# Routing an expert layer by bf16 one-hot matmuls, and one weight subtraction moved behind two products

## Chip, core and metric

The kernel runs on one core of a Trainium2 chip. Its time is the device time of one execution in microseconds (us), as the median over executions. TensorE (PE in the rows, its weight loads PEld), VectorE (DVE), ScalarE (ACT), GpSimd (POOL) and SyncE (SP) work side by side and wait for each other through semaphores.

## The reference

One layer over 1024 latent tokens of width 1024, with 256 context tokens in front. A token mixer (input projection, a spatial-gating half, a recurrent half, output projection) is followed by a mixture of 16 experts. All inputs are float32. What matters here is the second part:

```
aff = softmax(h @ w_r)                    # 1024 tokens x 16 experts
gate, idx = top_k(aff.T, 128)             # each expert chooses 128 tokens
xe = h[idx]
hid = silu(xe @ w1) * (xe @ w3)           # w1, w3: 1024 x 2048 for each expert
ye = (hid @ w2) * gate                    # w2: 2048 x 1024
out = rmsnorm(x + g2 * zeros.at[idx].add(ye))
```

## The kernel before

**First stages.** Up to about 430 us the kernel computes the modulation, the mixer and the router logits. Tiles that live through the kernel lie in the pool `con` on the left side of SBUF; the working tiles of these stages lie in pools on the right side, above a filler tile `edge_pad`. A second filler, `gap_pad`, lies on the left, just below the pool `mb` of the expert loop. The fillers are never used; they only set the addresses of what follows.

**Sorting and places.** Each expert's 128th largest score is found by a sort on VectorE, whose steps stand in the list `fills` and are issued one by one. From the thresholds, lines L1189 to L1205 compute `pos`: the place (0 to 127) that a token has in an expert's list, or a number out of range.

**Routing.** `route_oh(e)` compares `pos` with 0..127 on VectorE, which gives eight one-hot blocks of 128 x 128 in fp32r. `route(e)` multiplies them, as stationary operands, with `tvr`: for each token and expert four fp32r columns (token number, score rounded to fp32r, the rest of the score, token number again). The eight matmuls add up in PSUM; VectorE turns column 0 into an integer (L1230) and adds columns 1 and 2 into the gate (L1231). GpSimd then gathers the rows with an indirect DMA.

**Expert loop.** Weights come in pieces of 1 MB (128 x 2048, float32), 24 for each expert, into a ring of 12 buffers, by DMAs that SyncE issues as buffers come free. ScalarE rounds a piece to fp32r (`hi`, L107), VectorE subtracts (`lo`, L109), and TensorE multiplies hi by hi, hi by lo and lo by hi (L1258, L1260, L1262 in `up`; L1301, L1304, L1307 in `down`). The split of a piece is issued two pieces ahead (`presplit`, LA = 2), into three buffers for `hi` and `lo`. For each expert e the order is `up("3", e)`, `hidden(e)`, `up("1", e + 1)`, `down(e)`. `up` fills four PSUM banks over eight pieces; in its first piece it takes the banks in two halves, (0, 1) and (2, 3). `hidden` multiplies the four banks with the stored silu on VectorE, and so frees them. Since TensorE has six banks in all, the second half of the next `up` needs two banks that `hidden` frees. `route(e + 2)` is issued after piece 6 of `up("3", e)`. So the order on VectorE around that place is: subtractions of pieces up to the next `up`'s piece 0, the two small operations of `route`, the subtraction of piece 1, four products, the subtractions of pieces 2 and 3.

Of the kernel before, what the change touches and what calls it, by code (L numbers as in the profile page):

```python
# [7 lines left out]
F32 = mybir.dt.float32  # L8
F32R = mybir.dt.float32r
BF = mybir.dt.bfloat16  # L10
I32 = mybir.dt.int32
AF = mybir.ActivationFunctionType
OP = mybir.AluOpType
AX = mybir.AxisListType
# [4 lines left out]
NE = 16  # L19
FE = 2048  # L20
P = 128
# [3 lines left out]
LA = 2  # L25
# [20 lines left out]
def hybrid_layer(ctx, tc, x, c, ctxt, c_ctx, w_mod, b_mod, norm1_g, norm2_g, w_in, sgu_g, sgu_w,  # L46
# [3 lines left out]
    V, A, PE, G = nc.vector, nc.scalar, nc.tensor, nc.gpsimd  # L50
# [7 lines left out]
    con = ctx.enter_context(tc.tile_pool(name="con", bufs=1))  # L58
# [11 lines left out]
    def bank(shape, name, small=0):  # L70
        return banks[small].tile(shape, F32, name=name, tag="bk")
# [30 lines left out]
    def presplit(n, eng, pool=None, defer=None):  # L102
        while nsplit[0] < min(len(units), n):
            s = units[nsplit[0]][1]
            hi = (pool or sp).tile([P, 2048], F32R, name="hi")
            lo = (pool or sp).tile([P, 2048], F32R, name="lo")
            A.activation(hi, s, AF.Copy)  # L107
            if defer is None:
                eng.tensor_tensor(lo, s, hi, op=OP.subtract)  # L109
            else:  # L110
                defer.append(lambda lo=lo, s=s, hi=hi: eng.tensor_tensor(lo, s, hi, op=OP.subtract))
            ready[nsplit[0]] = (hi, lo)
            nsplit[0] += 1

    def unit(key):
        n = nused[0]
        nused[0] += 1
        assert units[n][0] == key
        presplit(n + 1 + LA, V)
        return ready.pop(n)  # L120

    plan("1", w1, 0)
# [3 lines left out]
    ph1 = ExitStack()  # L126
    wbs, bps, p0s = ExitStack(), ExitStack(), ExitStack()
    edge = wbs.enter_context(tc.tile_pool(name="edge", bufs=1, side="right"))
    edge.tile([P, 56], F32, name="edge_pad")
    wb = wbs.enter_context(tc.tile_pool(name="wb", bufs=2, side="right"))  # L130
    bp = bps.enter_context(tc.tile_pool(name="bp", bufs=1, side="right"))
    p0 = p0s.enter_context(tc.tile_pool(name="p0", bufs=1, side="right"))
# [30 lines left out]
    for q in range(4):  # L163
# [9 lines left out]
    iota_s = con.tile([P, P], F32, name="iota_s")  # L173
    G.iota(iota_s, pattern=[[1, P]], base=0, channel_multiplier=0,
           allow_small_or_imprecise_dtypes=True)
    tv = con.tile([P, 8, NE, 2], F32, name="tv")
    G.iota(tv[:, :, :, 0], pattern=[[P, 8], [0, NE]], base=0, channel_multiplier=1,
           allow_small_or_imprecise_dtypes=True)
    for r0, n_, src in ((72, 8, rg_lam.rearrange("o d (b p) -> (o d b) p", p=P)),
                        (80, 8, rg_ba.rearrange("o d (b p) -> (o d b) p", p=P)),  # L180
                        (88, 8, rg_bi.rearrange("o d (b p) -> (o d b) p", p=P)),
# [119 lines left out]
    for k in range(8):  # L301
        hi = p0.tile([P, 2048], F32R, name="mhi", bufs=2)
        lo = p0.tile([P, 2048], F32R, name="mlo", bufs=2)
        for c0, n_ in (((0, 4),) if k < 7 else ((0, 1), (1, 1), (2, 1), (3, 1))):
# [3 lines left out]
            for w in (hi, lo):  # L308
                for n in range(c0, c0 + n_):
                    PE.matmul(pm[n], cs4[:, k, :], w[:, n * 512:(n + 1) * 512],  # L310
                              start=(k == 0 and w is hi), stop=(k == 7 and w is lo))
# [18 lines left out]
    for j in range(16):  # L330
# [8 lines left out]
                           op0=OP.add, op1=OP.mult)  # L339
# [343 lines left out]
    pr = ph1.enter_context(tc.tile_pool(name="pr", bufs=1))  # L683
# [160 lines left out]
    p = bank([P, 4, P], "ws")  # L844
# [30 lines left out]


    pes = ExitStack()
    pe_ = pes.enter_context(tc.tile_pool(name="pe", bufs=1, side="right", reuse_waits="tile"))

    A2 = pe_.tile([P, D], F32, name="A2row")  # L880
# [16 lines left out]
    def x_load(t):  # L897
        XR[t] = pe_.tile([P, D], F32, name="xr", bufs=2)
        nc.sync.dma_start(XR[t], x[t * P:(t + 1) * P])

    x_load(0)
    x_load(1)
    affs = tv[:, :, :, 1]

    groups = ((0,), (1, 2), (3, 4), (5,), (6, 7))
    WS, SS = [[pe_.tile([64, 64], F32, name=f"{c_}{i}") for i in range(2)] for c_ in "WS"]
# [3 lines left out]
    V.tensor_scalar(tri, jp, 0.0, None, op0=OP.is_gt)  # L910
    oneb = pe_.tile([P, P], BF, name="oneb")
    G.memset(oneb, 1.0)
    for v in pre:
        G.memset(v, 0.0)
    def out_mm(t, h, ks=range(4), ns=(0, 1)):
# [15 lines left out]
    fills = []  # L931
# [14 lines left out]
    def wait2():  # L946
        fills.append(done2[0] + len(fills2))
# [62 lines left out]
    def router_w(t):  # L1010

        i = [t == g_[-1] for g_ in groups]
        if not any(i):
            return
        i = i.index(True)
        n = NE * len(groups[i])
        pt = bank([n, P], "pt")
        PE.transpose(pt, affs[:, groups[i][0]:t + 1].rearrange("p t e -> p (t e)"), ident)
        for h in range(2):
            A.activation(WS[i][32 * h:32 * h + n], pt[:, h * 64:(h + 1) * 64], AF.Copy)  # L1020
# [48 lines left out]
    for t in range(1, 8):  # L1069
# [4 lines left out]
        if t in (4, 6):  # L1074
            i = t // 2 - 1
# [59 lines left out]
    fill(1)  # L1135
    ph1.close()

    tvr = ctx.enter_context(tc.tile_pool(name="tvp", bufs=1)).tile([P, 8, NE, 4], F32R, name="tvr")
    sp = ctx.enter_context(tc.tile_pool(name="sp", bufs=LA + 1))
    res_add(7, 1)  # L1140
    nc.sync.dma_start(x2d[7 * P:], xr)
# [19 lines left out]
    del fills[:]  # L1161
    router_sm(7)
    router_w(7)
    A.activation(tvr[:, :, :, 1], affs, AF.Copy)
    for i in (0, 3):
        A.activation(tvr[:, :, :, i], tv[:, :, :, 0], AF.Copy)
    q_sort(4, L5)
    LZ = LS[0]
    fills.insert(8, lambda: V.tensor_sub(tvr[:, :, :, 2], affs, tvr[:, :, :, 1]))
    wait2()  # L1170
    q_merge(LS[1], L5, LZ)
    while fills:
# [36 lines left out]
    mp = ctx.enter_context(tc.tile_pool(name="mp", bufs=1))  # L1209
    xe, ix, xT, sg, hT = {}, {}, {}, {}, {}  # L1210

    OH = {}

    def route_oh(e):
        oh = mp.tile([P, 8, P], F32R, name="oh", tag="xe", bufs=2)
        n = 1 if e else 2
        for h in range(n):
            ts = slice(8 // n * h, 8 // n * (h + 1))
            V.tensor_tensor(oh[:, ts], iota_s[:, None, :].to_broadcast([P, 8 // n, P]),
                            pos[:, ts, e:e + 1].to_broadcast([P, 8 // n, P]), op=OP.is_equal)  # L1220
        OH[e] = oh

    def route(e):
        oh = OH.pop(e)
        p = bank([P, 4], "pr", 1)
        for t in range(8):
            PE.matmul(p, oh[:, t], tvr[:, t, e, :], start=(t == 0), stop=(t == 7))
        i = mp.tile([P, 1], I32, name="ix", bufs=4)
        g = mp.tile([P, 1], F32, name="gate", bufs=4)
        V.tensor_copy(i, p[:, 0:1])  # L1230
        V.tensor_reduce(g, p[:, 1:3], axis=AX.X, op=OP.add)  # L1231
        if e == NE - 1:
            V.tensor_copy(ixf, p[:, 0:1])
        ix[e] = (i, g)
        xe[e] = mp.tile([P, D], F32, name="xe", bufs=2)
        G.indirect_dma_start(out=xe[e], out_offset=None, in_=hx2d,  # L1236
                             in_offset=bass.IndirectOffsetOnAxis(ap=i[:, :1], axis=0))
# [13 lines left out]
    def up(which, e, mid):  # L1251
        pt = [bank([P, 512], "h" + which) for _ in range(4)]
        hi, lo = xT[e]
        for k in range(8):
            wh, wl = unit((which, e, k))
            for bs in (((0, 1), (2, 3)) if k == 0 else ((0, 1, 2, 3),)):
                for b in bs:
                    PE.matmul(pt[b], hi[:, k], wh[:, b * 512:(b + 1) * 512], start=(k == 0), stop=False)  # L1258
                for b in bs:
                    PE.matmul(pt[b], hi[:, k], wl[:, b * 512:(b + 1) * 512], start=False, stop=False)  # L1260
                for b in bs:
                    PE.matmul(pt[b], lo[:, k], wh[:, b * 512:(b + 1) * 512], start=False, stop=(k == 7))  # L1262
            if k in mid:
                mid[k]()
        return pt
# [10 lines left out]
    def hidden(e, pt):  # L1276
        for b in range(4):
            s = sg[e][b]
            V.tensor_mul(s, s, pt[b].rearrange("t (p j) -> t j p", j=4))  # L1279

    def transpose_h(e, bs):
        for b in bs:
# [56 lines left out]
    route_oh(1)  # L1339
    p1 = up("1", 0, {2: lambda: route(1)})  # L1340
    gap = ctx.enter_context(tc.tile_pool(name="gap", bufs=1))
    gap.tile([P, 32], F32, name="gap_pad")
    mb = ctx.enter_context(tc.tile_pool(name="mb", bufs=1))
    silu(0, p1)
    ixf = mp.tile([P, 1], F32, name="ixf")
    for e in range(NE):
        nxt = e + 1 < NE
        if nxt:
            load("1", w1, e + 1)
        if e < NE - 2:  # L1350
            load("2", w2, e)
        if nxt:
            load("3", w3, e + 1)
        if e == NE - 2:
            load("2", w2, e)
        if not nxt:
            load("2", w2, e)
        mid = {}
        if nxt:
            mid[2] = lambda: transpose_x(e + 1)  # L1360
        if e + 2 < NE:
            mid[3] = lambda: route_oh(e + 2)
            mid[6] = lambda: route(e + 2)
        if nxt:
            hidden(e, up("3", e, mid))
            p1 = up("1", e + 1, {2: lambda: transpose_h(e, (0, 1)), 4: lambda: transpose_h(e, (2, 3))})
            if e + 2 < NE:
                down(e, {u: lambda b=b: silu1(e + 1, p1, b) for b, u in enumerate((0, 2, 4, 6))})
            else:
                silu(e + 1, p1)  # L1370
        else:
            A.preload_act_table_set("sqrt_and_others")
            iw = mp.tile([P, S], F32, name="iw", tag="xe", bufs=2)
            G.iota(iw, pattern=[[1, S]], base=0, channel_multiplier=0, allow_small_or_imprecise_dtypes=True)
            ohT = mp.tile([P, S], F32R, name="ohT", tag="xth")
            V.tensor_scalar(ohT, iw, ixf, None, op0=OP.is_equal)
            fg = mp.tile([P, D], F32, name="fg", tag="xe", bufs=2)
            row_bcast(fg, fgc)
            hidden(e, up("3", e, mid))
            down(e - 1, {u: lambda b=b: transpose_h(e, (b,)) for b, u in enumerate((1, 3, 5, 7))})  # L1380
# [131 lines left out]
```

## Time and profile before

| | |
|---|---|
| median of three executions | 1621.77 us (1614.16 to 1622.4) |
| the profiled execution | 1619.82 us, span 1617.7 us |
| TensorE busy (matmul / weight load) | 1531.9 us (95%) / 1257.4 us (78%) |
| VectorE, ScalarE, GpSimd busy | 1386.6 (86%), 1089.8 (67%), 144.6 us (9%) |
| mean granted TensorE clock | 0.974 |
| DMA | 485.30 MB, mean 300 GB/s |

Busy time of TensorE counts pipelined matmuls by their modelled ends, so 95% does not say that nothing could go between them; the distance between the starts of matmuls does. The chain that ended last says which work, step by step, set the end.

### The profile page before, as it was taken

The page shows a single profiled execution, that of the slowest core. Times are in us where ns is not written, and L with a number is a line of the kernel's source. Part 1 is how long each engine was busy: PE and PEld are TensorE (multiplying, and loading weights), DVE is VectorE, ACT ScalarE, POOL GpSimd, SP SyncE. Part 2 cuts the span into 40 slices and gives each one's busy share as a digit, 9 for nine tenths or more (in the row PEclk, how much of TensorE's full clock was granted, in tenths as well). Part 3 has the DMA queues.
Part 4 walks back from the last instruction along what each step waited for, and adds up shares of the span by engine and source line. Part 5 has one row for each costly group of instructions (what it writes and reads, how often), then busy time and mean ns, then how long its engine had stood idle before and what let it go on. Part 6 is the DMA issues. An engine that isn't in the chain of part 4 may idle for free.

```text
span 1617.7 us, 19119 instructions
## 1 busy us (share of the span) xinstructions
PE 1531.9 (95%) x7288; PEld 1257.4 (78%) x7288; DVE 1386.6 (86%) x1322; ACT 1089.8 (67%) x990; POOL 144.6 (9%) x126
## 2 busy tenths in 40 slices
PE   5899989999769999999999999999999999999996
PEld 2687779888657888888888888888888888887784
DVE  6668788886878898998989889898998989889797
ACT  6577654722347877777777777868777787777873
POOL 2411121000010010010100001010010100001002
PEclk8899999998879999999999999999999999999998
DMA  9110147435659999999999999999999999999855
GB/s 383 35 36 30 66 151 228 171 127 207 233 214 357 381 375 356 396 366 397 381 365 381 372 378 381 380 385 357 387 370 388 387 371 373 370 384 377 325 173 207
DMA packets 85947, 485.30 MB, mean 300 GB/s; under 512 B 11224, under 2 KB 20064, under 8 KB 35680
## 3 DMA queue, kind: packets, MB, share of 16 engines
q1 hardware_dynamic: 80896, 466.72, 74.9%
q0 software_dynamic: 4864, 17.34, 4.3%
q8 instruction: 57, 0.93, 0.2%
q14 instruction: 34, 0.28, 0.0%
q10 hardware_dynamic: 96, 0.03, 0.0%
HBM read 463.61 MB, written 20.45 MB: 299 GB/s over the span
## 4 chain that ended last, share of the span: by engine, by line
PE 67%; DVE 16%; ACT 7%; DMA 7%; issue 3%; POOL 1%; SPq 0%; DVEq 0%; POOLq 0%; ACTq 0%
PE h L1258 12%; PE h L1262 12%; PE h L1260 12%; PE ye L1304 7%; PE ye L1301 7%; PE ye L1307 7%; DMA raw<-in_w_dram 3%; DVE lo L109 3%; ACT hi L107 2%; PE hp L1285 2%; DVE ring L404 1%; DMA ring<-in_w_mod_dram 1%; DVE sg L1279 1%; PE pw L925 1%; PE pw L927 1%
## 5 line engine op out<-in xcount | busy, mean ns | idle before, releaser
L109 DVE TENSOR_TENSOR lo<-raw,hi 128x2048 fp32r<-128x2048 f32 x383 | 871.0, 2292 | 116.3 <-ACT hi L107 112.1
L107 ACT ACTIVATE hi<-raw 128x2048 fp32r<-128x2048 f32 x384 | 737.3, 1922 | 215.5 <-PE h L1262 150.9
L1258 PE MATMUL h<-hi,xth 128*128 128x512 f32 x1024 | 292.6, 400 | 3.6 <-ACT sg L1269 1.2
L1260 PE MATMUL h<-lo,xth 128*128 128x512 f32 x1024 | 279.9, 390 | 1.9 <-DVE lo L109 1.9
L1262 PE MATMUL h<-hi,xtl 128*128 128x512 f32 x1024 | 279.7, 390 | 0.0
L1258 PEld LDWEIGHTS h<-hi,xth 128*128 128x128 f32 x1024 | 187.8, 188 | 50.6 <-DVE sg L1279 12.6
L1260 PEld LDWEIGHTS h<-lo,xth 128*128 128x128 f32 x1024 | 192.4, 188 | 42.6 <-DVE lo L109 2.8
L1262 PEld LDWEIGHTS h<-hi,xtl 128*128 128x128 f32 x1024 | 192.4, 188 | 40.6
L1301 PE MATMUL ye<-hi,hth 128*128 128x512 f32 x512 | 158.0, 390 | 0.0
L1304 PE MATMUL ye<-lo,hth 128*128 128x512 f32 x512 | 157.8, 389 | 0.0
L1307 PE MATMUL ye<-hi,htl 128*128 128x512 f32 x512 | 157.6, 389 | 0.0
L1317 POOL DMA_INDIRECT x2d<-ye,ix x15 | 50.6, 3374 | 790.0 <-DVE ye L1314 790.0
L1304 PEld LDWEIGHTS ye<-lo,hth 128*128 128x128 f32 x512 | 96.0, 188 | 20.3 <-DVE lo L109 0.3
L1307 PEld LDWEIGHTS ye<-hi,htl 128*128 128x128 f32 x512 | 96.1, 188 | 20.0
L1301 PEld LDWEIGHTS ye<-hi,hth 128*128 128x128 f32 x512 | 95.8, 188 | 19.6
L1269 ACT ACTIVATE sg<-h 128x512 f32<-128x512 f32 x64 | 69.7, 1109 | 0.1
L1288 ACT ACTIVATE hth<-hp 128x512 fp32r<-128x512 f32 x64 | 35.0, 596 | 42.3 <-PE hp L1285 42.3
L377 PE MATMUL pu<-hxh,wh 128*128 128x512 f32 x128 | 51.0, 399 | 1.0 <-ACT g1row L738 1.0
L1236 POOL DMA_INDIRECT xe<-hx2d,ix x16 | 17.7, 1106 | 382.9 <-DVE gate L1231 367.5
L379 PE MATMUL pu<-hxl,wh 128*128 128x512 f32 x128 | 50.6, 395 | 0.0
L378 PE MATMUL pu<-hxh,wl 128*128 128x512 f32 x128 | 50.6, 395 | 0.0
L404 DVE SCALAR_TENSOR_TENSOR ring<-ring,cs 128x1024 f32<-128x1024 f32 x28 | 42.2, 1506 | 8.0 <-DMA ring<-in_w_mod_dram 7.3
(346 smaller groups left out, 1897.5 us busy)
## 6 DMA issues: line engine op xcount, KB each, us to landing
raw<-in_w_dram SPq DMA_DIRECT2D x383, 1024.0 KB, 7.6
ring<-in_w_mod_dram SPq DMA_DIRECT2D x32, 512.0 KB, 4.9
wmod<-in_w_mod_dram SPq DMA_DIRECT2D x8, 1024.0 KB, 10.6
wraw<-in_w_in_dram SPq DMA_DIRECT2D x6, 1024.0 KB, 11.9
xh<-in_x_dram SPq DMA_DIRECT2D x4, 1024.0 KB, 15.7
wor<-in_w_out_dram SPq DMA_DIRECT2D x4, 1024.0 KB, 8.5
xr<-in_x_dram SPq DMA_DIRECT2D x8, 512.0 KB, 4.1
x2d<-xr SPq DMA_DIRECT2D x8, 512.0 KB, 3.5
```

Of the source, the lines that this page charges most:

```text
L107: A.activation(hi, s, AF.Copy)
L109: eng.tensor_tensor(lo, s, hi, op=OP.subtract)
L377: PE.matmul(p, w[0][:, k], act[0][:, k], start=(k == 0), stop=False)
L378: PE.matmul(p, w[1][:, k], act[0][:, k], start=False, stop=False)
L404: V.scalar_tensor_tensor(macc, row, cs[:, k, 0:1], macc, op0=OP.mult, op1=OP.add)
L1258: PE.matmul(pt[b], hi[:, k], wh[:, b * 512:(b + 1) * 512], start=(k == 0), stop=False)
L1260: PE.matmul(pt[b], hi[:, k], wl[:, b * 512:(b + 1) * 512], start=False, stop=False)
L1262: PE.matmul(pt[b], lo[:, k], wh[:, b * 512:(b + 1) * 512], start=False, stop=(k == 7))
L1269: A.activation(s.rearrange("t j p -> t p j"), pt[b].rearrange("t (p j) -> t p j", j=4), AF.Silu)
L1301: PE.matmul(pt[n], hi[:, j], wh[:, j2 * 1024 + n * 512:j2 * 1024 + n * 512 + 512], start=st_, stop=False)
L1304: PE.matmul(pt[n], hi[:, j], wl[:, j2 * 1024 + n * 512:j2 * 1024 + n * 512 + 512], start=False, stop=False)
L1307: PE.matmul(pt[n], lo[:, j], wh[:, j2 * 1024 + n * 512:j2 * 1024 + n * 512 + 512], start=False, stop=en)
```

## The change

The score of a token is split into three bf16 parts instead of two fp32r parts, and its number into two (128 t, and the row within the block). `tvr` holds these five columns in bf16, and the one-hot is written in bf16, so that the eight matmuls of a `route` run in bf16. VectorE adds the two number columns in PSUM (f), copies f to an integer, and adds three columns for the gate. The last expert's f serves where `ixf` was copied before. The split of the scores takes two subtractions and one more rounding in the sort's list; the columns with the numbers are filled earlier. In `up("3", e)` the subtraction for the piece that is split at k = 7 (piece 1 of what comes next) is held in the list `LOW` and issued inside `hidden`, behind the second product. The fillers change size, and one is added.

```diff
-    def unit(key):
+    LOW = []
+
+    def unit(key, late=False):
...
-        presplit(n + 1 + LA, V)
+        presplit(n + 1 + LA, V, defer=LOW if late else None)
...
-    edge.tile([P, 56], F32, name="edge_pad")
+    edge.tile([P, 40], F32, name="edge_pad")
...
-    tv = con.tile([P, 8, NE, 2], F32, name="tv")
-    G.iota(tv[:, :, :, 0], pattern=[[P, 8], [0, NE]], base=0, channel_multiplier=1,
+    affs = con.tile([P, 8, NE], F32, name="affs")
...
+    edge2.tile([P, 48], F32, name="edge2_pad")
...
+    place = pe_.tile([P, 8, NE, 2], F32, name="place")
+    G.iota(place[:, :, :, 0], pattern=[[P, 8], [0, NE]], base=0, channel_multiplier=0,
+    G.iota(place[:, :, :, 1], pattern=[[0, 8], [0, NE]], base=0, channel_multiplier=1,
...
-    tvr = ctx.enter_context(tc.tile_pool(name="tvp", bufs=1)).tile([P, 8, NE, 4], F32R, name="tvr")
+    tvr = tvp.tile([P, 8, NE, 6], BF, name="tvr")
+    rest = tvp.tile([P, 8, NE], F32, name="rest")
+    A.activation(tvr[:, :, :, 0:2], place, AF.Copy)
...
-    A.activation(tvr[:, :, :, 1], affs, AF.Copy)
-    for i in (0, 3):
-        A.activation(tvr[:, :, :, i], tv[:, :, :, 0], AF.Copy)
+    A.activation(tvr[:, :, :, 2], affs, AF.Copy)
...
-    fills.insert(8, lambda: V.tensor_sub(tvr[:, :, :, 2], affs, tvr[:, :, :, 1]))
+    fills.insert(6, lambda: (V.tensor_sub(rest, affs, tvr[:, :, :, 2]),
+                             A.activation(tvr[:, :, :, 3], rest, AF.Copy)))
+    fills.insert(12, lambda: V.tensor_sub(tvr[:, :, :, 4], rest, tvr[:, :, :, 3]))
...
-        oh = mp.tile([P, 8, P], F32R, name="oh", tag="xe", bufs=2)
+        oh = mp.tile([P, 16, P], BF, name="oh", tag="xe", bufs=2)[:, :8]
...
-            PE.matmul(p, oh[:, t], tvr[:, t, e, :], start=(t == 0), stop=(t == 7))
+            PE.matmul(p[:, :5], oh[:, t], tvr[:, t, e, :5], start=(t == 0), stop=(t == 7))
...
-        V.tensor_copy(i, p[:, 0:1])
-        V.tensor_reduce(g, p[:, 1:3], axis=AX.X, op=OP.add)
-        if e == NE - 1:
-            V.tensor_copy(ixf, p[:, 0:1])
+        V.tensor_reduce(f, p[:, 0:2], axis=AX.X, op=OP.add)
+        V.tensor_copy(i, f)
+        V.tensor_reduce(g, p[:, 2:5], axis=AX.X, op=OP.add)
+        IXF[0] = f
...
-            wh, wl = unit((which, e, k))
+            wh, wl = unit((which, e, k), which == "3" and k == 7)
...
             V.tensor_mul(s, s, pt[b].rearrange("t (p j) -> t j p", j=4))
+            if b == 1:
+                while LOW:
+                    LOW.pop(0)()
...
-    gap.tile([P, 32], F32, name="gap_pad")
+    gap.tile([P, 40], F32, name="gap_pad")
...
-    ixf = mp.tile([P, 1], F32, name="ixf")
```

## Rows read from the trace of the kernel before

**Rows 1.** The page's chain by engine; one stretch of the loop (us, busy by engine).
```profile
PE 67%; DVE 16%; ACT 7%; DMA 7%; issue 3%; POOL 1%; SPq 0%; DVEq 0%; POOLq 0%; ACTq 0%
...
715.00:780.00 65.00, 64.90 (x301) 53.55 (x300) 59.03 (x37) 48.06 (x31) 4.35 (x2) 1.00 1.00 392
```

**Rows 2.** The chain (start us, us, what) around `route` and `hidden`, expert 5.
```profile
860.93 1.93 ACT hi L107
...
865.14 1.28 DVE sg L1279 x2
866.46 0.50 PE h L1258
```

**Rows 3.** TensorE's timeline there (start us, us, engine, line, operation).
```profile
860.73 0.95 PE L1227 MATMUL pr<-tvr,oh 128*128 128x4 f32 x8
861.54 1.19 PE L1258 MATMUL h<-hi,xth 128*128 128x512 f32 x4
...
863.49 1.08 PE L1262 MATMUL h<-hi,xtl 128*128 128x512 f32 x4
864.40 0.62 PE L1258 MATMUL h<-hi,xth 128*128 128x512 f32 x2
...
867.73 1.07 PE L1258 MATMUL h<-hi,xth 128*128 128x512 f32 x4
```

**Rows 4.** VectorE's timeline of the same stretch.
```profile
855.86 6.69 DVE L109 TENSOR_TENSOR lo<-raw,hi 128x2048 fp32r<-128x2048 f32 x3
862.47 0.15 DVE L1230 CAST ix<-pr 128x1 int32<-128x1 f32 x1
...
862.88 2.33 DVE L109 TENSOR_TENSOR lo<-raw,hi 128x2048 fp32r<-128x2048 f32 x1 [0.19 <-ACT hi L107]
865.14 2.47 DVE L1279 TENSOR_TENSOR sg<-sg,h 128x512 f32<-128x512 f32 x4
```

**Rows 5.** Eight transposes on TensorE and ScalarE's reading of both their banks.
```profile
848.96 1.04 PE L1246 MATMUL xp<-ident,xe 128*128 128x128 f32 x8
...
849.60 1.09 ACT L1247 ACTIVATE xth<-xp 128x512 fp32r<-128x512 f32 x2 [1.25 <-PE xp L1246]
```

**Rows 6.** The same place of expert 14 (no `route`), and expert 15's `down`.
```profile
1489.43 0.61 PE L1258 MATMUL h<-hi,xth 128*128 128x512 f32 x2
...
1493.66 1.07 PE L1258 MATMUL h<-hi,xth 128*128 128x512 f32 x4
...
1546.40 0.30 PEld L1304 LDWEIGHTS ye<-lo,hth 128*128 128x128 f32 x2 [0.29 <-DVE lo L109]
```

**Rows 7.** Timeline and window of the first routing: bf16 and fp32r matmuls.
```profile
455.58 0.31 PE L1198 MATMUL pq<-pre,tri 128*128 128x128 bf16 x1
...
455.68 0.31 PE L1199 MATMUL pq<-pre,oneb 128*128 128x128 bf16 x1
...
456.85 1.29 DVE L1219 TENSOR_TENSOR oh<-iota_s,pos 128x512 fp32r<-128x512 f32 x2
...
457.64 1.84 PE L1227 MATMUL pr<-tvr,oh 128*128 128x4 f32 x8 [1.54 <-DVE oh L1219]
...
459.34 1.97 PE L736 MATMUL rb<-ident,mcol 128*128 128x128 f32 x8
...
456.00:458.00 2.00, 0.46 (x3) 0.39 (x3) 1.85 (x5) 0.00 (x0) 0.00 (x0) 0.50 0.00 0
```

**Rows 8.** VectorE's timeline in the last sort: the scores' subtraction.
```profile
443.34 0.37 DVE L1169 TENSOR_TENSOR tvr<-tv,tvr 128x128 fp32r<-128x128 f32 x1
```

**Rows 9.** By source line: weight DMAs, their landing, conversions and subtractions (ns min/median/max).
```profile
L91 SPq DMA_DIRECT2D raw<-in_w_dram x383: 327/328/749, 363.1 to 1548.6; - x192
...
L107 ACT ACTIVATE hi<-raw x384: 1901/1921/1936, 461.8 to 1577.6; 128x2048 fp32r<-128x2048 f32 x192
...
L109 DVE TENSOR_TENSOR lo<-raw,hi x383: 2277/2292/2341, 463.8 to 1579.6; 128x2048 fp32r<-128x2048 f32 x192
...
DMA to landing us min/median/max: 5.0/7.6/17.7
```

More of the change, by code (lines that the diff above doesn't have):

```diff
@@ L175, in hybrid_layer @@
            allow_small_or_imprecise_dtypes=True)
-    tv = con.tile([P, 8, NE, 2], F32, name="tv")
-    G.iota(tv[:, :, :, 0], pattern=[[P, 8], [0, NE]], base=0, channel_multiplier=1,
-           allow_small_or_imprecise_dtypes=True)
+    affs = con.tile([P, 8, NE], F32, name="affs")
     for r0, n_, src in ((72, 8, rg_lam.rearrange("o d (b p) -> (o d b) p", p=P)),
@@ L877, in hybrid_layer @@
     pes = ExitStack()
+    edge2 = pes.enter_context(tc.tile_pool(name="edge2", bufs=1, side="right"))
+    edge2.tile([P, 48], F32, name="edge2_pad")
     pe_ = pes.enter_context(tc.tile_pool(name="pe", bufs=1, side="right", reuse_waits="tile"))
@@ L902, in hybrid_layer @@
     x_load(1)
-    affs = tv[:, :, :, 1]
     groups = ((0,), (1, 2), (3, 4), (5,), (6, 7))
@@ L912, in hybrid_layer @@
     G.memset(oneb, 1.0)
+    place = pe_.tile([P, 8, NE, 2], F32, name="place")
+    G.iota(place[:, :, :, 0], pattern=[[P, 8], [0, NE]], base=0, channel_multiplier=0,
+           allow_small_or_imprecise_dtypes=True)
+    G.iota(place[:, :, :, 1], pattern=[[0, 8], [0, NE]], base=0, channel_multiplier=1,
+           allow_small_or_imprecise_dtypes=True)
     for v in pre:
@@ L1136, in hybrid_layer @@
     ph1.close()
-    tvr = ctx.enter_context(tc.tile_pool(name="tvp", bufs=1)).tile([P, 8, NE, 4], F32R, name="tvr")
+    tvp = ctx.enter_context(tc.tile_pool(name="tvp", bufs=1))
+    tvr = tvp.tile([P, 8, NE, 6], BF, name="tvr")
+    rest = tvp.tile([P, 8, NE], F32, name="rest")
+    A.activation(tvr[:, :, :, 0:2], place, AF.Copy)
     sp = ctx.enter_context(tc.tile_pool(name="sp", bufs=LA + 1))
@@ L1210, in hybrid_layer @@
     xe, ix, xT, sg, hT = {}, {}, {}, {}, {}
-    OH = {}
+    OH, IXF = {}, {}
     def route_oh(e):
-        oh = mp.tile([P, 8, P], F32R, name="oh", tag="xe", bufs=2)
+        oh = mp.tile([P, 16, P], BF, name="oh", tag="xe", bufs=2)[:, :8]
         n = 1 if e else 2
@@ L1224, in route @@
         oh = OH.pop(e)
-        p = bank([P, 4], "pr", 1)
+        p = bank([P, 6], "pr", 1)
         for t in range(8):
-            PE.matmul(p, oh[:, t], tvr[:, t, e, :], start=(t == 0), stop=(t == 7))
+            PE.matmul(p[:, :5], oh[:, t], tvr[:, t, e, :5], start=(t == 0), stop=(t == 7))
         i = mp.tile([P, 1], I32, name="ix", bufs=4)
-        g = mp.tile([P, 1], F32, name="gate", bufs=4)
-        V.tensor_copy(i, p[:, 0:1])
-        V.tensor_reduce(g, p[:, 1:3], axis=AX.X, op=OP.add)
-        if e == NE - 1:
-            V.tensor_copy(ixf, p[:, 0:1])
+        gf = mp.tile([P, 2], F32, name="gate", bufs=4)
+        g, f = gf[:, 0:1], gf[:, 1:2]
+        V.tensor_reduce(f, p[:, 0:2], axis=AX.X, op=OP.add)
+        V.tensor_copy(i, f)
+        V.tensor_reduce(g, p[:, 2:5], axis=AX.X, op=OP.add)
+        IXF[0] = f
         ix[e] = (i, g)
@@ L1375, in hybrid_layer @@
             ohT = mp.tile([P, S], F32R, name="ohT", tag="xth")
-            V.tensor_scalar(ohT, iw, ixf, None, op0=OP.is_equal)
+            V.tensor_scalar(ohT, iw, IXF[0], None, op0=OP.is_equal)
             fg = mp.tile([P, D], F32, name="fg", tag="xe", bufs=2)
```

## The prediction

> **What bounds the kernel now.** I read the page's chain by engine first: TensorE is on it for 67% of the span, VectorE for 16%, ScalarE for 7% [rows 1]. Then one stretch of the expert loop (the window row gives its length, the busy time of TensorE, its weight loads, VectorE, ScalarE and GpSimd, the granted clock, the DMA share and GB/s): clock 1.00, VectorE 59 of 65 us, DMA share 1.00 [rows 1]. So TensorE runs at its full 2.4 GHz there, and VectorE and DMA are close behind; whether either holds it up must be read from waits.
>
> The chain shows one place in each expert where TensorE does not set the pace [rows 2]: a rounding on ScalarE at 860.93, the subtraction of that piece, two products of `hidden` at 865.14, and only then a matmul at 866.46. TensorE's timeline of the same place gives the size [rows 3]. Four matmuls take 0.91 us (863.49 to 864.40), so a piece of twelve takes 2.72. The first piece of `up("1")`, begun at 864.40, is followed by the second at 867.73: 3.33, so 0.61 is lost to the wait for two banks. In front of it, `route`'s eight matmuls take 0.81 us (860.73 to 861.54). They lie beside the chain of ScalarE and VectorE, not on it: shortening them alone would bring nothing. That decides how the two halves of the change must be counted, the products first.
>
> The ring of weights is no bound. The last piece is issued at 1548.6 and first used at 1577.6, 29 us later, and a transfer lands 7.6 us after its issue (median), 17.7 at most [rows 9]. Some 21 us, and at least 11, are in hand.
>
> **The products before the subtraction.** Let t0 be the start of the last group of `up("3")`, 863.49 [rows 3]. The first product needs only its own bank. That such a wait ends bank by bank is seen at the transposes: ScalarE reads at 849.60, while the eight transposes last to 850.00 [rows 5]. The first bank's matmul lasts 1.08 - 3 x 0.227 = 0.40 us, and the chain shows 0.04 us from VectorE's end to TensorE (865.14 + 1.28 to 866.46 [rows 2]); so the first product starts at t0 + 0.45. Four products last 2.47 [rows 4] and two 1.28 [rows 2], so each moves the next by 0.60; three subtractions last 6.69 and one 2.29 [rows 4, 9], so each moves the next by 2.20. With the held subtraction in the middle, VectorE ends the subtraction for piece 2 at 0.45 + 4 x 0.60 + 2 x 2.20 + 0.09 = t0 + 7.34; TensorE can take it at 7.38. The banks are free at t0 + 1.1 and 1.7, before the second half of the piece wants them at 2.27: the 0.61 goes. What is late next is piece 2: its second group is due at 0.91 + 2 x 2.72 + 0.91 = t0 + 7.26, so 0.12 to 0.13 us of wait stays. Piece 1 has its subtraction at t0 + 3.9 and wants it at 4.5.
>
> VectorE must be free for the first product. Its three subtractions end at 862.55, `route`'s small operations follow (0.15 us each [rows 4]); a third one that waits for the first adds 0.1 to 0.3, to 863.0 or so, against 863.55 (t0 already moved up by 0.4, below).
>
> Gain, experts 0 to 13: 14 x (0.61 - 0.13) = 6.7 us. Expert 14 has no `route` to hide under; its piece takes 4.23 (1489.43 to 1493.66 [rows 6]), 1.51 over, so 1.4 is gained. Expert 15 goes on to `down`, which needs no freed banks; TensorE waits there for the third subtraction already [rows 6], and VectorE now begins later: minus 0.1, at worst the 0.6 of a whole such wait.
>
> **bf16 matmuls in `route`.** No row shows a bf16 matmul at full clock. At the first routing the clock is 0.50, 1.2 GHz, and both kinds stand there [rows 7]: fp32r one-hots follow each other at (459.34 - 457.64) / 8 = 0.21 us, bf16 128 x 128 matmuls at 0.10 (455.58 to 455.68). With four columns moving, the fp32r distance can only be the weight load's, so bf16 halves it. In the loop that is half of 0.81: 0.40 us for each route. Once the wait of `hidden` is gone, TensorE is what ends last there, and the 0.40 counts. Fifteen routes at full clock (1 to 15): 6.0 us. Bounds: below, 0, if the distance at full clock is not the load's (a loss is excluded by the two distances); above, the whole 0.81, 12.2.
>
> The Trainium skill says more (TensorE: Matmul & The Clock Gate, "Weight-path perf modes"): a load of 128 columns in a type other than fp32 is read in a faster way by itself, measured at about twice. The bf16 rows can't show it, since 128 columns move in each of those matmuls. By the halved distance the sum is 1606, by this rule some 1603; it is a rival below, worked out from rows.
>
> Route 0 runs at half clock on the chain. Its eight matmuls would end 0.86 us earlier, but the second half of the one-hot is ready only at 456.85 + 1.29 = 458.14 [rows 7], so they end at about 458.6 instead of 459.34; the extra operation on VectorE takes 0.2 back: 0.5 us. The one-hot compare itself keeps float32 inputs and its duration; were it slower by a third, VectorE's free time in front of the first product (0.5 us) would cover it.
>
> **The rest.** One more subtraction in the sort, where VectorE works alone: 0.4 us lost [rows 8]; ScalarE's roundings there lie beside it. The two iotas run on GpSimd, and the early fill of the number columns on ScalarE while TensorE still multiplies; 0. The fillers: 512 bytes less on the left, 64 less on the right, then 192 more, all multiples of 64. That addresses change a duration is not seen: 383 subtractions in twelve ring buffers last 2277 to 2341 ns [rows 9]. I take 0, and 1% of the first 300 us, 3 us either way, as bounds. The last expert's copy and the second number column were never on the path.
>
> **Sum**, against the profiled execution's 1619.82 us (span 1617.7): 6.7 + 1.4 - 0.1 + 6.0 + 0.5 - 0.4 = 14.1, so 1605.7. The median of the runs shown is 1.95 us above the profiled one, and the runs span 1614 to 1622; I stay with 1606.
>
> **Rivals.**
> - Only one half pays. If bf16 does not shorten `route`, 6.7 + 1.4 - 0.1 - 0.4 = 7.6 stays: 1612. If the wait moves whole to piece 2, only the routes count, at most 6.1: 1614. For: no row shows either at full clock. Against: the halved distance, and 0.13 of wait where 0.61 would be needed. Chance 0.17.
> - The faster load. If the bf16 load takes half of the distance in rows 7, a route saves 0.20 more, 15 x 0.20 = 3.0: 1603. Chance 0.08. This is what the Trainium skill's rule above would do here.
> - The transfers are the bound. The DMA share is 1.00 [rows 1], and the loop would have to move the same bytes 1.2% faster. If it can't, nothing is gained: 1620. Against: 14 us over the loop is less than the 21 us in hand [rows 9], so even a fixed rate would hardly show. Chance 0.08.
> - Slower: the first product waits for a later signal of TensorE than its own bank's, as the end of the six matmuls that need no freed bank, and starts at t0 + 2.4. Then the banks come free at t0 + 3.1 instead of 2.27, the subtraction for piece 2 at 9.3 instead of 7.26, and TensorE loses some 2.1 us for each expert instead of 0.61; less 0.40 for the route, 15 x 1.1 = 16 us more: 1636. It turns from gain to loss where the first product starts later than t0 + 1.3 (wait 1.01 = 0.61 + 0.40). Against: rows 5. Chance 0.07.
>
> **Numbers.** The forecast has 0.60. About 0.5%, 8 us, is what a measurement of this kernel can tell from no change, so faster means below 1611.7. It holds 0.95 of the forecast, all of the faster load, and 0.35 of the one half: 0.57 + 0.08 + 0.06 = 0.71. Same: 0.03 + 0.11 + 0.07 (transfers) = 0.21. Slower 0.08. The range 1600 to 1615 takes in the address bound, the faster load and most of the one-half cases; outside lie the transfers, the late signal and the tails.
>
> **What would show it.** Right: in TensorE's rows, `route` takes about 0.4 us, the piece after `hidden` 2.72, no weight load waits for a product, and the next piece's second group waits about 0.1 for a subtraction; from transposes to transposes an expert takes 0.9 us less. Wrong: the wait stands at piece 2 in full size (VectorE's budget was miscounted), `route`'s matmuls keep 0.1 us between starts, conversions wait for landings, or the first 440 us differ by more than 3 us (addresses do matter).

## The result, and the profile after

The changed kernel takes 1600.85 us, median of 4 runs (1597.47 to 1605.19), where the kernel before, beside it, takes 1620.8: a ratio of 0.9878, 95% interval 0.9855 to 0.9902. The forecast was 1606, faster. The profiled execution has a span of 1595.4 us against 1617.7.

The span, the busy times and the chain by engine, which answer to [rows 1]:

```profile
span 1595.4 us, 19136 instructions
...
PE 1511.7 (95%) x7288; PEld 1241.8 (78%) x7288; DVE 1384.2 (87%) x1338; ACT 1091.2 (68%) x990; POOL 144.6 (9%) x127
...
PE 75%; DVE 13%; ACT 5%; DMA 4%; issue 2%; POOL 1%; SPq 0%; DVEq 0%; POOLq 0%; ACTq 0%
```

TensorE now has 75% of the chain instead of 67. The chain cut to one stretch with the same place of expert 5 has no engine but TensorE in it, where [rows 2] had a rounding, a subtraction and two products:

```profile
by line: PE h L1270 32.5%; PE h L1268 30.8%; PE h L1272 30.4%; PE xp L1256 2.9%; PE hp L1298 2.9%; PE pr L1236 0.7%
```

TensorE's timeline of that place, to be laid beside [rows 3]; t0 is 851.35:

```profile
849.20 0.35 PE L1236 MATMUL pr<-tvr,oh 128*128 128x5 bf16 x8
849.41 1.18 PE L1268 MATMUL h<-hi,xth 128*128 128x512 f32 x4
...
851.35 1.08 PE L1272 MATMUL h<-hi,xtl 128*128 128x512 f32 x4
852.27 0.62 PE L1268 MATMUL h<-hi,xth 128*128 128x512 f32 x2
...
854.99 1.07 PE L1268 MATMUL h<-hi,xth 128*128 128x512 f32 x4
...
857.71 1.07 PE L1268 MATMUL h<-hi,xth 128*128 128x512 f32 x4
858.73 1.19 PE L1270 MATMUL h<-lo,xth 128*128 128x512 f32 x4
859.76 1.09 PE L1272 MATMUL h<-hi,xtl 128*128 128x512 f32 x4
860.69 1.04 PE L1298 MATMUL hp<-ident,sg 128*128 128x128 f32 x8
```

`route`'s eight matmuls take 0.21 us (849.20 to 849.41) instead of 0.81. The first piece after `hidden` takes 2.72 (852.27 to 854.99) instead of 3.33, and so does the next. The third takes 2.98 (857.71 to 860.69): 0.26 is what is left of the wait. VectorE's timeline ([rows 4] before) says why:

```profile
844.34 6.69 DVE L109 TENSOR_TENSOR lo<-raw,hi 128x2048 fp32r<-128x2048 f32 x3
850.95 0.15 DVE L1240 TENSOR_REDUCE gate<-pr 128x1 f32<-128x2 f32 x1
...
851.20 0.15 DVE L1242 TENSOR_REDUCE gate<-pr 128x1 f32<-128x3 f32 x1
851.79 1.28 DVE L1289 TENSOR_TENSOR sg<-sg,h 128x512 f32<-128x512 f32 x2 [0.43 <-PE h L1272]
852.99 2.29 DVE L111 TENSOR_TENSOR lo<-raw,hi 128x2048 fp32r<-128x2048 f32 x1
855.19 1.28 DVE L1289 TENSOR_TENSOR sg<-sg,h 128x512 f32<-128x512 f32 x2
856.39 6.69 DVE L109 TENSOR_TENSOR lo<-raw,hi 128x2048 fp32r<-128x2048 f32 x3
```

VectorE is free 0.43 us ahead of the first product, which starts at 851.79, t0 + 0.44; the held subtraction (L111) stands between the pairs; the subtraction for piece 2, first of the last three, ends at 856.39 + 2.29 = 858.68, and TensorE takes it at 858.73. The waits of TensorE's weight loads between 500 and 1400 us (us in total, times, longest), where the kernel before had one such line, `h L1258 <- DVE sg L1279: 10.1, 26, 0.4`, are now

```profile
PEld h L1270 <- DVE lo L109: 4.8, 13, 0.4
PEld L1236 <- issue: 3.7, 14, 0.3
```

so no weight load waits for a product any more. Expert 14's wait for products is gone as well; its first piece takes 2.72. What is left on the weight loads there, two pieces later, and in expert 15's `down` ([rows 6] before), by their timeline, is

```profile
1475.62 0.76 PEld L1270 LDWEIGHTS h<-lo,xth 128*128 128x128 f32 x4 [0.38 <-DVE lo L109]
...
1524.93 0.30 PEld L1317 LDWEIGHTS ye<-lo,hth 128*128 128x128 f32 x2 [0.36 <-DVE lo L109]
```

The first routing ([rows 7] before), on TensorE:

```profile
451.62 0.25 PE L1236 MATMUL pr<-tvr,oh 128*128 128x5 bf16 x4 [1.54 <-DVE oh L1228]
452.18 0.27 PE L1236 MATMUL pr<-tvr,oh 128*128 128x5 bf16 x4 [0.31 <-DVE oh L1228]
452.31 1.95 PE L736 MATMUL rb<-ident,mcol 128*128 128x128 f32 x8
```

The transfers keep up. In the stretch of the loop that [rows 1] shows, the DMA share is still 1.00:

```profile
715.00:780.00 65.00, 65.00 (x300) 53.79 (x299) 59.70 (x36) 50.33 (x33) 4.23 (x2) 1.00 1.00 381
```

No weight load waits for a rounding between 500 and 1400 us. The view of waits puts 23 waits of ScalarE's roundings in that time down to a landing, 18.6 us in all (16 and 16.3 us before); nearly all are of 0.8 us, as long as those that it puts down to TensorE (at most 0.8), so they hold nothing up.

Where the 22.3 us between the two profiled spans went is read from two marks. From the first transposes `xp` to the last product with the gate (the `ye` of expert 15) it is 1120.33 us before (465.25 to 1585.58) and 1105.85 after (458.28 to 1564.13): 14.5 us in the loop. Ahead of it 7.0 are gained and behind it 0.85. How much of these two belongs to the kernel, and how much to the one execution, two traces can't tell, so the experiments are judged by this loop time, taken from their traces, beside their medians.

### The profile page after: what moved, and what is told of

Its sections match the earlier page's. It is cut to its first block, busy times and chain, and to the rows that moved or that the text cites. A ratio compares the mean times of both kernels' runs of the same rounds, so it can differ in the third digit from the quotient of the medians.

```text
span 1595.4 us, 19136 instructions
## 1 busy us (share of the span) xinstructions
PE 1511.7 (95%) x7288; PEld 1241.8 (78%) x7288; DVE 1384.2 (87%) x1338; ACT 1091.2 (68%) x990; POOL 144.6 (9%) x127
## 4 chain that ended last, share of the span: by engine, by line
PE 75%; DVE 13%; ACT 5%; DMA 4%; issue 2%; POOL 1%; SPq 0%; DVEq 0%; POOLq 0%; ACTq 0%
PE h L1270 14%; PE h L1268 14%; PE h L1272 14%; PE ye L1317 7%; PE ye L1314 7%; PE ye L1320 7%; PE hp L1298 2%; DMA ring<-in_w_mod_dram 2%; DVE ring L404 1%; PE xp L1256 1%; DMA ctx_sb<-in_ctx_dram 1%; DVE tm L967 1%; DMA wor<-in_w_out_dram 1%; PE pl L1004 1%; PE pw L931 1%
## 5 line engine op out<-in xcount | busy, mean ns | idle before, releaser
L109 DVE TENSOR_TENSOR lo<-raw,hi 128x2048 fp32r<-128x2048 f32 x367 | 830.9, 2289 | 95.5 <-ACT hi L107 93.1
L1268 PE MATMUL h<-hi,xth 128*128 128x512 f32 x1024 | 287.1, 397 | 1.2 <-ACT sg L1279 1.2
L1317 PEld LDWEIGHTS ye<-lo,hth 128*128 128x128 f32 x512 | 96.0, 188 | 20.3 <-DVE lo L109 0.4
L1279 ACT ACTIVATE sg<-h 128x512 f32<-128x512 f32 x64 | 69.7, 1109 | 0.1
L1246 POOL DMA_INDIRECT xe<-hx2d,ix x16 | 17.4, 1085 | 386.6 <-PE h L1272 242.5
```

Of the source, the lines that this page charges most:

```text
L1279: A.activation(s.rearrange("t j p -> t p j"), pt[b].rearrange("t (p j) -> t p j", j=4), AF.Silu)
L1317: PE.matmul(pt[n], hi[:, j], wl[:, j2 * 1024 + n * 512:j2 * 1024 + n * 512 + 512], start=False, stop=False)
```

## Experiments

Loop times in us. Three traces of the kernel before give 1120.33, 1120.53 and 1122.23, three of the changed one 1105.85, 1105.72 and 1105.74. With the two kernels that differ from the one before only ahead of the loop (`first_alone`, `first_again`) the old loop spreads over 2.2 us, about half of it in the stretch of expert 0. The period of a later expert, from its transposes `xp` to those of the next, repeats to some 0.1 us and is the sharper measure.

| kernel | median | ratio to before, 95% interval | loop |
|---|---|---|---|
| after_again | 1601.94 | 0.9872 [0.9851, 0.9893] | 1105.72 |
| after_third | 1601.75 | 0.9878 [0.9864, 0.9892] | 1105.74 |
| first_alone | 1618.1 | 0.9981 [0.9964, 0.9998] | 1121.18 |
| first_again | 1618.69 | 0.9986 [0.9967, 1.0005] | 1120.05 |
| defer_alone | 1614.89 | 0.9953 [0.9935, 0.9970] | 1114.97 |
| bf16_alone | 1616.04 | 0.9976 [0.9956, 0.9996] | 1119.14 |
| products_later | 1601.02 | 0.9863 [0.9844, 0.9881] | 1102.03 |
| held_last | 1612.68 | 0.9939 [0.9921, 0.9958] | 1114.43 |
| bf16_split | 1631.43 | 1.0053 [1.0037, 1.0070] | 1131.15 |
| load_96 | 1608.8, one run | | 1110.35 |

**The changed kernel again.**

> The changed kernel as it is, as the measure for the runs beside it. The traces of before and after put 15.3 us of the gain into the expert loop, 0.95 into the first routing and 6.2 into the stages before the sort, which do nearly the same work. Theory 1: the 6.2 us of the first stages are a difference between executions (runs of each kernel spread over 8 us), so over several rounds it is 15 to 17 us faster than the kernel before. Rival: the first stages gained from their new addresses, and it is 20 to 22 us faster.

> The changed kernel once more, as the one beside which the other three of this job are read. Every theory: 0.987 to 0.989 of the kernel before. From the first transposes xp to the last result of the experts 1105.5 to 1106.2 us, as in its two traces so far (1105.85 and 1105.72); what differs between executions lies before that, in the first 440 us.

`after_third` came out as expected, and the loop of the changed kernel repeats to 0.13 us over its three traces. `after_again` did not come out by its theory. Its time is the rival's: by the medians 20.3 us less than the kernel before, where the theory had 15 to 17, and the interval of its ratio (17.4 to 24.2 us) leaves the theory out. The other two measurements of the changed kernel say the same, 20.0 and 20.2 us by the medians. So some 4 us beyond the loop, the first routing and the sort come back in every round; they are not chance of one execution.

**Each half alone.** `defer_alone` is the kernel before with the held subtraction and nothing else:

```diff
-            wh, wl = unit((which, e, k))
+            wh, wl = unit((which, e, k), which == "3" and k == 7)
...
+            if b == 1:
+                while LOW:
+                    LOW.pop(0)()
```

> The kernel before with only the held subtraction. Theory 1: the wait for the two banks (0.61 us an expert, 1.5 in expert 14) goes, some 0.25 us of it comes back as a wait for piece 2's subtraction, and the 0.81 us of the fp32r route stays: 14 x 0.36 + 1.2 = 6 us faster. Rival (the two halves add up freely, and the deferral is worth only what the bf16 routes leave of 15.3, some 6 too) does not differ here; it differs in the bf16 half alone.

`bf16_alone` is the changed kernel without it (the bf16 routes and the new places stay):

```diff
-            wh, wl = unit((which, e, k), which == "3" and k == 7)
+            wh, wl = unit((which, e, k))
```

> The changed kernel without the held subtraction: the subtraction stands in front of all four products again. Theory 1: the shorter route lies beside the chain of rounding, subtraction and products, so TensorE waits as much longer as the route is shorter: the wait for the banks grows from 0.61 to 1.2 us an expert, and only the first routing's 0.95 less 0.2 for the sort is left: 1 us faster than before (plus what the first stages bring, if anything). Rival (the halves add up): 15 x 0.60 + 0.7 = 10 us faster.

Measured: the loop is 5.4 us shorter with the held subtraction alone, 1.2 with bf16 alone (less than the old kernel's loop times differ among themselves), 14.5 with both. So the halves don't add: bf16 is worth 9.1 us once the products come first (1114.97 to 1105.85), and nearly nothing without. Both theories hold; the rival's 10 us for bf16 alone lie outside its interval (0.6 to 7.1 us). TensorE's timeline of `bf16_alone` at the same place shows where it goes:

```profile
859.49 0.61 PE L1268 MATMUL h<-hi,xth 128*128 128x512 f32 x2
...
860.39 0.61 PE L1272 MATMUL h<-hi,xtl 128*128 128x512 f32 x2
861.51 1.09 PE L1268 MATMUL h<-hi,xth 128*128 128x512 f32 x2 [0.51 <-DVE sg L1289]
...
863.37 1.07 PE L1268 MATMUL h<-hi,xth 128*128 128x512 f32 x4
```

The piece takes 3.88 us (859.49 to 863.37), 1.16 over the 2.72, where it was 0.61 over in [rows 3]. `route` is 0.60 shorter, and nearly all of it stands in the wait for the two products behind it. Expert 5's period there is 69.50 us, as good as the 69.54 of the kernel before; in `defer_alone` it is 69.21, in the changed kernel 68.58. So by the expert 0.04 and 0.33 us are gained alone, and 0.96 together.

**Where the held subtraction stands.** `held_last` has it behind all four products:

```diff
-            if b == 1:
+            if b == 3:
```

> The changed kernel with the held subtraction behind all four products instead of behind two. Theory (VectorE's order sets it): the subtraction for piece 1 ends 1.2 us later, at t0 + 0.45 + 4 x 0.60 + 2.2 = t0 + 5.1, and is wanted at t0 + 4.5: a wait of 0.6 at piece 1; the subtraction for piece 2 ends when it did (t0 + 7.3 to 7.5) while piece 2 now begins 0.6 later, so its wait of 0.26 goes. Net 0.3 to 0.4 us for each expert, 14 x 0.35 = 5 us more in the loop: 1111. Rival (the place inside the products does not matter, since VectorE's whole work there is the same): the loop stays at 1105.8.

Measured: 8.7 us more in the loop than the changed kernel; the direction and the place are the theory's, the size was 5. The rival, that the place inside the products doesn't matter, falls. TensorE's timeline there:

```profile
867.67 1.07 PE L1268 MATMUL h<-hi,xth 128*128 128x512 f32 x4
869.21 1.20 PE L1270 MATMUL h<-lo,xth 128*128 128x512 f32 x4 [0.47 <-DVE lo L111]
...
871.16 1.07 PE L1268 MATMUL h<-hi,xth 128*128 128x512 f32 x4
```

Piece 1 waits, takes 3.49 us instead of 2.72 and so costs 0.77; the 0.26 of piece 2 is saved; 14 x 0.51 = 7.1 is most of the 8.7; most of the rest is in expert 15's `down`, which waits 1.3 us for the held subtraction instead of 0.36, by the waits of the weight loads from 1400 to 1560 us:

```profile
PEld ye L1317 <- DVE lo L111: 1.3, 1, 1.3
```

In the rows of expert 5 the second matmul group starts 0.63 late (869.21 against 868.58), as expected; the rest of the 0.77 is behind it: 1.03 to the next group instead of 0.91.

**Two products behind the next subtraction.** `products_later` moves products 2 and 3 behind the subtraction for piece 2 (`product` holds the two lines of one product):

```diff
-        for b in range(4):
-            s = sg[e][b]
-            V.tensor_mul(s, s, pt[b].rearrange("t (p j) -> t j p", j=4))
-            if b == 1:
-                while LOW:
-                    LOW.pop(0)()
+        for b in range(2):
+            product(e, pt, b)
+        while LOW:
+            LOW.pop(0)()
+        HID.extend(lambda b=b: product(e, pt, b) for b in (2, 3))
...
     def unit(key, late=False):
...
         presplit(n + 1 + LA, V, defer=LOW if late else None)
+        while HID:
+            HID.pop(0)()
```

> The changed kernel with products 2 and 3 of hidden behind the subtraction for piece 2 instead of ahead of its third in the queue. Theory: what is left at this place is the 0.26 us by which that subtraction ends late; two products of 0.6 us fewer stand ahead of it, so it ends 1.2 us earlier and the wait goes, while products 2 and 3 are still done well before their transposes. 14 or 15 experts times 0.26 = 3.6 to 3.9 us less in the loop, about 1102 from the first xp to the last ye. Rival: the place is limited by something else of TensorE (the weights' load of that group, seen as a longer first matmul), then nothing is gained: 1105.8. Second rival: the two products now end too late for the freed banks of pieces that want banks 2 and 3 (they are wanted 2.27 us after t0, and come only after the subtraction, at about t0 + 6): then each expert loses some 3 us and the loop is 40 us longer, 1147.

Measured: 1102.03, 3.7 us less in the loop, as the theory had it; both rivals fall. TensorE's timeline of the piece that had kept 0.26:

```profile
865.30 1.07 PE L1270 MATMUL h<-hi,xth 128*128 128x512 f32 x4
866.20 1.07 PE L1272 MATMUL h<-lo,xth 128*128 128x512 f32 x4
...
868.03 1.03 PE L1303 MATMUL hp<-ident,sg 128*128 128x128 f32 x8
```

865.30 to 868.03 is 2.73. VectorE's rows show the two subtractions ahead of the second pair of products:

```profile
860.58 2.29 DVE L111 TENSOR_TENSOR lo<-raw,hi 128x2048 fp32r<-128x2048 f32 x1
862.78 2.29 DVE L109 TENSOR_TENSOR lo<-raw,hi 128x2048 fp32r<-128x2048 f32 x1
864.98 1.28 DVE L1290 TENSOR_TENSOR sg<-sg,h 128x512 f32<-128x512 f32 x2
```

By the loop this version beats both kernels. By whole runs the difference to the changed kernel can't be told: the ratios 0.9863 and 0.9878 have overlapping intervals, for 3.7 us is less than executions of one kernel differ in the first stages (below).

**The bf16 load.** Was the rival of the faster load right, by which only a full set of 128 columns is read faster? `bf16_split` divides each matmul into 96 and 32 columns:

```diff
-            PE.matmul(p[:, :5], oh[:, t], tvr[:, t, e, :5], start=(t == 0), stop=(t == 7))
+            PE.matmul(p[:96, :5], oh[:, t, :96], tvr[:, t, e, :5], start=(t == 0), stop=(t == 7))
+            PE.matmul(p[96:, :5], oh[:, t, 96:], tvr[:, t, e, :5], start=(t == 0), stop=(t == 7))
```

> The changed kernel with each of route's bf16 matmuls split in two, of 96 and 32 columns of weights, the same result. In the change one of 128 columns takes 26 ns from start to start, a quarter of the fp32r one's 101. Theory 1 (the whole 128 columns of bf16 are what is loaded faster, and narrower loads go at half the fp32r's time for a column, 0.40 ns): 8 x (38 + 13 to 26) ns = 0.41 to 0.51 us for a route instead of 0.21, so 0.2 to 0.3 us more for each of 15 routes, 3 to 4.5 us more in the loop: 1109 to 1110. Theory 2 (every bf16 load is four times as fast as an fp32r one): 8 x (20 + 7) ns = 0.21, nothing more, 1105.8. Theory 3 (26 ns is a least distance of two matmuls and not the load's time): 16 x 26 ns = 0.42 us, 3 us more, and the two halves of a pair have equal distances.

A miss for all three theories: 25.4 us more in the loop. TensorE's timeline of one route:

```profile
868.27 0.17 PE L1236 MATMUL pr<-tvr,oh 128*96 128x5 bf16 x1
868.37 0.18 PE L1237 MATMUL pr<-tvr,oh 128*32 128x5 bf16 x1
868.48 0.21 PE L1236 MATMUL pr<-tvr,oh 128*96 128x5 bf16 x1
...
870.19 1.20 PE L1269 MATMUL h<-hi,xth 128*128 128x512 f32 x4
```

It takes 1.92 us (868.27 to 870.19): 0.10 to 0.14 from each start to the next, which swallows any difference between loads. The Trainium skill has a reason (TensorEngine Tiling (Array Packing), "Key Properties"): a change of the array's tiling mode drains TensorE. The rows agree with a cost at each change between these two forms. They don't show the drain as such, nor that 96 and 32 columns are two modes; and the one change from 96 to 128 columns in the next kernel shows no such cost.

`load_96` puts eight matmuls of one width, 96 columns, ahead of each route's own eight:

```diff
+        for t in range(8):
+            PE.matmul(p[:96, :5], oh[:, t, :96], tvr[:, t, e, :5], start=(t == 0), stop=(t == 7))
         for t in range(8):
             PE.matmul(p[:, :5], oh[:, t], tvr[:, t, e, :5], start=(t == 0), stop=(t == 7))
```

> The changed kernel with eight more bf16 matmuls ahead of each route, of 96 columns of weights in place of 128, all of one width; their result is written over by the eight that follow. It measures the bf16 load without changing width at every matmul, as the split kernel did. Theory 1 (only the whole 128 columns load fast; a narrower load goes at half the fp32r's time for a column): the eight start 38 to 40 ns apart, 0.30 us. Theory 2 (the load of bf16 is as fast whatever its width): 20 to 27 ns apart, 0.16 to 0.21 us. Theory 3 (any width under 128 is a change of the array's form, with which no load runs beside a matmul): 0.1 us or more apart, as in the split kernel, 0.8 us or more.

TensorE's timeline of one route has both kinds side by side:

```profile
857.89 0.48 PE L1236 MATMUL pr<-tvr,oh 128*96 128x5 bf16 x8
858.24 0.34 PE L1238 MATMUL pr<-tvr,oh 128*128 128x5 bf16 x8
858.44 1.16 PE L1270 MATMUL h<-hi,xth 128*128 128x512 f32 x4
```

Eight of 96 columns take 0.35 us, 44 ns each; eight of 128 take 0.20, 25 ns each. Fewer columns load more slowly: theory 1, with 44 instead of 38 to 40. By the column that is 0.46 ns against 0.20, and 0.79 for fp32r (0.81 us / 8 / 128): nearly the halving that [rows 7] let expect, and on top of it a further factor of 2.3 for the full width. That is the rule of the Trainium skill that the prediction weighed (TensorE: Matmul & The Clock Gate, "Weight-path perf modes"), and the trace agrees with it in what loads faster.

Are the 25 ns the load's own time? The same trace has both kinds at half clock, in route 0 (the window's row gives the clock, 0.50):

```profile
458.57 0.48 PE L1236 MATMUL pr<-tvr,oh 128*96 128x5 bf16 x4
458.91 0.35 PE L1238 MATMUL pr<-tvr,oh 128*128 128x5 bf16 x8
459.12 0.45 PE L736 MATMUL rb<-ident,mcol 128*128 128x128 f32 x1
...
458.00:459.20 1.20, 1.08 (x17) 1.01 (x18) 0.51 (x1) 0.00 (x0) 0.00 (x0) 0.50 0.00 0
```

There the matmuls of 96 columns are 85 ns apart, about twice the 44, but those of 128 are 26 ns apart, as at full clock. So the distance at 96 columns follows the clock, and the one at 128 does not: at full clock something other than the load, a least distance of two matmuls, is likely what sets the 25 ns (the part of theory 3 of `bf16_split` that this bears out). At half clock the full width is four times as fast by the column (0.21 against 0.89 ns), where the Trainium skill's section has about twice; the 2.3 at full clock is only the least that the load can have gained.

**The first stages.** `first_alone` and `first_again` are the kernel before with the new tile places ahead of the loop alone:

```diff
-    edge.tile([P, 56], F32, name="edge_pad")
+    edge.tile([P, 40], F32, name="edge_pad")
...
-    tv = con.tile([P, 8, NE, 2], F32, name="tv")
...
+    affs = con.tile([P, 8, NE], F32, name="affs")
...
+    edge2 = pes.enter_context(tc.tile_pool(name="edge2", bufs=1, side="right"))
+    edge2.tile([P, 48], F32, name="edge2_pad")
...
+    place = pe_.tile([P, 8, NE, 2], F32, name="place")
```

> The kernel before with only the new places of tiles in the first stages: the scores in a tile of their own, the token numbers made later, both right-hand fillers as in the changed kernel; routing and loop as before. Theory 1 (addresses and the moved iotas cost nothing): same as before, within 2 us. Rival (the first stages gained): 4 to 6 us faster.

> The kernel before with the new tile places in the first stages alone, once more. Theory (the new places are worth some 3 us): a ratio of 0.997 to 0.999, and a clock of 1.00 from 360 to 380 us. Rival (the first measurement was at the edge by chance, the places are worth nothing): 1.000, its interval with values on both sides.

> The kernel before once more, for its trace. Theory (the fall of the granted clock near 365 us belongs to the old places of the first stages' tiles): the granted clock of 360 to 380 us is below 0.9 again, as in both traces with these places so far (0.83 and 0.74). Rival (it is chance, one execution in some): 1.00 there. From the first xp to the last ye 1120 to 1121.5 us in any case.

> As the run ahead of it: by the theory the clock of 360 to 380 us is below 0.9 in each execution with the old places; by the rival it is 1.00 in some of them.

By the ratios the places are worth 3.1 us in the first measurement and 2.3 in the second. The first interval leaves out "no gain" by a hair (0.9998), the second takes it in (1.0005). The windows from 360 to 380 us (busy by engine, granted clock, DMA share, GB/s) of before_again, first_again and held_last, one fence each:

```profile
360.00:380.00 20.00, 20.00 (x100) 17.29 (x99) 12.59 (x37) 5.01 (x14) 0.00 (x0) 0.83 0.52 199
```

```profile
360.00:380.00 20.00, 20.00 (x115) 17.31 (x114) 13.77 (x44) 4.88 (x14) 0.00 (x0) 1.00 0.54 205
```

```profile
360.00:380.00 20.00, 19.13 (x96) 16.35 (x95) 13.28 (x35) 6.15 (x16) 0.00 (x0) 0.83 0.55 211
```

With the old places the clock is 0.74 or 0.83 there in all four traces. With the new ones it is 1.00 in six (first_again is one) and 0.74 or 0.83 in four (products_later, held_last, bf16_split, load_96), though up to there these ten issue the same instructions. So the theory that the fall belongs to the old places is refuted; that they make it more frequent stays open. The values are means of the two levels. In before_again the clock is at half for six of the 20 us and a little more, while TensorE is busy all the time:

```profile
370.00:376.00 6.00, 6.00 (x19) 5.10 (x19) 3.65 (x7) 1.52 (x4) 0.00 (x0) 0.50 0.80 333
```

The last transposes of the router (`pt`) start at 440.3 to 443.2 us with the old places and at 434.0 to 444.5 with the new, and the fall goes with a late start: 440.3 or later in the eight traces that have it, 439.8 or earlier in the six that don't. So the 6.2 us between the two profiled executions say little of the kernel: executions with the new places alone differ by 10. The 0.85 behind the loop is the same kind of thing, by the windows of the same work in the kernel before and in the changed one:

```profile
1588.50:1591.50 3.00, 3.00 (x8) 2.42 (x8) 2.40 (x4) 1.45 (x3) 0.00 (x0) 0.50 0.01 3
```

```profile
1566.50:1569.50 3.00, 3.00 (x12) 2.10 (x13) 2.90 (x5) 1.22 (x3) 0.00 (x0) 1.00 0.02 8
```

After the same idle time of TensorE (1.28 us) it ran at half clock in the one and at full clock in the other; before_third, the old kernel, has the short tail too (31.28 us from the last `ye`, as after).

## Why the prediction was right, and which terms were off

- **The mechanism held.** The first product starts at t0 + 0.44 (0.45 predicted), the 0.61 goes, piece 2 is what is late next, and shortening `route` alone brings nothing, because it lies beside the chain from ScalarE over VectorE to the products. `bf16_alone` shows the last in one number: a period of 69.50 against 69.54.
- **The wait left at piece 2 was under-sized: 0.26 us, not 0.13.** The subtraction ends at t0 + 7.33 (7.34 predicted), and TensorE takes it 0.12 late, as forecast. The missing 0.14 is behind it: the next group follows after 1.03 us instead of 0.91 (858.73 to 859.76), and its weights are loaded only from 858.73 on, after the wait. In these rows a wait costs its own length and the cover of the load that waits with it; `held_last` shows the same 1.03. So the term 14 x 0.48 = 6.7 is 14 x 0.35 = 4.9. Expert 14 gains 1.25 instead of 1.4: its first piece loses the whole 1.51, but the same 0.26 stays two pieces later. With expert 15's minus 0.1 (0.36 against 0.29) that makes 6.1 us; `defer_alone` shows 5.4 against the first trace of before, and 6.1 against the mean of the three.
- **The bf16 routes were under-sized: 0.60 us each, not 0.40.** The rival of the faster load, given 0.08, had the size right: 15 x 0.60 = 9.0, and the loop shows 9.1. Only 14 of the routes can be seen in it: experts 1 to 14 gain some 0.62 each in their periods, 8.7 in all, and the other 0.4 lies in the stretch of expert 0, within its spread. The error lay in taking the halved distance of [rows 7], where 128 columns move, for the load's. `load_96` confirms the rule at its edge, the width, and at half clock, where the rival's price was 50 ns, a matmul takes 26.
- **These two nearly cancel in the loop:** 14.0 predicted (6.7 + 1.4 - 0.1 + 6.0), 14.5 measured by the two profiled executions, 15.3 by the means of three traces each. That the sum is so near is luck: one term is some 2 us too high, the other 3 too low.
- **Route 0: 0.95 instead of 0.5.** From `pr` to the first `xp` 6.66 us instead of 7.61. As predicted the second half of the one-hot decides (0.31 of wait at 452.18), but four matmuls behind it take 0.13, the fast load again, and the extra VectorE operation shows 0.06 instead of 0.2.
- **The sort: 0.2 lost instead of 0.4.** From `pt` to the first `pr` 17.60 instead of 17.37.
- **The first stages were put at 0, with 3 either way for addresses, and some 4 us are gained outside the loop, the first routing and the sort.** This is the largest term that the prediction missed. The new places alone give 2.3 or 3.1 us, not shown beyond doubt, and through what is not known.
- **The rivals.** One half only, the transfers and the late signal of TensorE are excluded by the rows above: no weight load waits for a product or for a rounding, `route` takes 0.21, and the first product starts as soon as its own bank is done.

The prediction had 14.1 us of gain; by the medians it is 20. Of the 6 between them, 1.3 lie in the loop (by the means), 0.65 in the first routing and the sort (0.45 + 0.2), and some 4 in the first stages and behind the loop. The new places of the tiles are the likely cause of 2 or 3 of these, and the rest isn't settled. The measured 1600.85 lies 0.85 above the lower end of the range, so the range held by the 3 us that it allowed for addresses and for the faster load, not by the sum.

## To carry to other kernels

Count two shortenings together: one off the path is worth nothing until the other has removed the wait that hides it, and then its whole length; here, by the expert, 0.33 and 0.04 us alone, 0.96 together. To see which comes first, ask in each place which engine ends last, and after a fix ask again; the next late operation was 0.26 us, and two products moved behind it removed that too. Where a trace has a spread of several us in one stage, judge a change in another by marks around it: 3.7 us were plain in the loop and invisible in the medians.

## What was not expected of the hardware

- A bf16 matmul of 96 columns of weights and five moving ones takes 44 ns from start to start at full clock and 85 at half, one of 128 columns 25 to 26 at either.
- Alternating widths of 96 and 32 takes 0.10 to 0.14 us for each matmul.
- The granted clock fell to 0.74 or 0.83 in the window from 360 to 380 us in some executions of one and the same sequence and not in others. In before_again it fell though TensorE was busy without a break from 340 to 380 us. Why it falls was not found.
